# Two fused transformer blocks on one core: query norm and rotation on VectorE, low-rank queries behind their projection, and other heads' work in front of the diff heads' transposes in the last stage

## The chip, the core and the metric

The kernel runs on one core of one Trainium2 chip. The core has TensorE (PE, the matrix engine), VectorE (DVE), ScalarE (ACT), GpSimd (POOL) and SyncE (SP, which here only issues DMAs). Each engine runs its own list of instructions strictly in order and waits where an operand isn't there yet. The metric is the time of one execution on the device, in microseconds (us); lower is better. The kernel before takes 1979.63 us, the median of 3 runs (1977.76 to 1987.02).

## What is computed

A first block (gated linear attention, spatial gating, a PEER layer with 16 of 16384 experts for each of 8 heads) is followed by a second one, which takes its output as x, a context of 256 tokens, and two conditioning vectors. There are 256 tokens, a width of 1024 and one batch entry. The change is in the second block, of two layers (DEPTH_2 = 2), and there in the latent tokens x alone, not in the context tokens:

```python
mod = silu_c @ w_ada[l] + b_ada[l]             # shifts, scales and gates
h = _rms(x, g_attn_pre[l]) * (1.0 + sc_a) + sh_a
p = h @ w_in                                   # q_a, kv_a, dq, dk, dv, gq, gk, gv
q = (_rms(q_a, g_mla_q) @ w_mla_qb)            # MLA: 4 heads of 64 + 32, rank 256
kv = (_rms(c_kv, g_mla_kv) @ w_mla_kvb)
q_d = _rope(dq, rope_small)                    # diff: 4 heads of 2 x 32
q_g = _rope(_rms(gq, g_gqa_q), rope_large)     # GQA: 8 query heads of 64
k_g = _rope(_rms(gk, g_gqa_k), rope_large)     #      2 key heads
o = softmax(q @ [k, k_ctx].T * scale) @ [v, v_ctx]
d = _rms(o_diff[0] - lam * o_diff[1], g_diff_sub) * (1.0 - lam_init)
x = x + gt_a * _rms(concat(o_mla, d, o_gqa) @ w_out[l], g_attn_post[l])
hf = _rms(x, g_ffn_pre[l]) * (1.0 + sc_f) + sh_f
x = x + gt_f * _rms((silu(hf @ w_gate) * (hf @ w_up)) @ w_down, g_ffn_post[l])
```

`_rope` multiplies the two halves of a head, x1 and x2, with tables: (x1 c - x2 s, x2 c + x1 s). `_rms` divides by the root of the mean square and multiplies by the gain.

## The kernel before

**Stages.** The first block comes first, with the context's layer 0 beside its PEER stage. The last stage, from about 1182 us, is the latent tokens' layer 0 (beside it the ada vectors of layer 1 and the context's keys of layer 1) and then layer 1. In both, `split` and `rope` are true: every operand of a large matmul is split in two float32r numbers, a high and a low one (`whi` and `wlo` of a weight, made by a cast on ScalarE at L188 and a subtraction on VectorE at L190; `bTh` and `bTl` of an activation, L365 and L370), and three matmuls take the place of one (L206).

**A layer.** `layer` norms and transposes x (L385, L395), and then projects in four blocks: A of the keys (`w2a`), A of the queries (`w2c`, first half: q_a and dq), B of the queries (`w2c`, second half: gq, in tile `qB`), and B of the keys and values (`w2b`, tile `kB`, named `kBx` in the profile for the latent tokens). Between them stand the diff heads' rotations and stacked operands (`qdS`, `kdS`), the MLA's low-rank queries (`lowrank`: norm, transposes `lr` at L1015; the load of `wqb`; matmuls `qb` at L1184; rotation; transposes into `qmT`), the MLA's keys (`kvb`, transposes into `kmT`) and the GQA queries (`gqa`: norm, rotation, transposes into `qgT`). Then `attention` runs 4 diff heads beside 2 pairs of MLA heads and 4 pairs of GQA heads: S by matmul, its maximum on VectorE (L1231), exponential on ScalarE (L1233), transposes PT (L1261), products `pd` (L1296) or `po` (L1330). At the diff heads' end comes a norm on VectorE (`dd`, L1350 and L1351) and transposes `ddT` (L1355). The output projection (`w2o`), a norm with a gate row (broadcast by 8 matmuls `bc`, L349, to a row `gv`), and the FFN follow: 22 tiles `ft` of 128 hidden units, each with gate and up matmuls (`gu`) and down products (`f`) into four banks, one per token tile t and half b.

**Who does what.** `GQ_POOL = 1` puts the norm's multiplies (L1031 gain, L1032 rstd) and the rotation (L984 to L990) of the 8 GQA query heads on GpSimd in the split layers. The power in `rstd` (L320) is on GpSimd wherever it has at most 16 columns.

**What sets the order.** Each piece is a Python generator that yields an estimate of its time; `together` and `merge` always advance the one that is behind. `ORDER = 2` picks the branch of `kv_gen` in which the low-rank queries run beside projection B of the keys. The framework's scheduler then arranges each engine's instructions by its own model of their times, within the dependences; `pinned` forbids single matmuls to move ahead of another. DMAs of weights are issued on SP in order, into four buffers (`raw`); a load waits until the last reader of its buffer is done. The loads of `wqb`, the keys' and queries' weights, the ada weights and `w2o` share these four.

**The last products.** With `STAGF = 3` the down products of token tile 1 for the last three ft are held back to the end; there they run ft by ft, both banks of each.

## Time and profile before

| | |
|---|---|
| median of 3 runs | 1979.63 us (1977.76 to 1987.02) |
| profiled execution | 1979.57 us, span 1977.8 us |
| busy PE, DVE, ACT, POOL | 1532.2 (77%), 1461.5 (74%), 691.4 (35%), 596.7 us (30%) |
| mean granted clock of TensorE | 0.876 |
| layer 0 of the last stage | about 1182 to 1582 us |
| layer 1 of the last stage | about 1582 us to the end |
| the chain that ended last | PE 46%, DVE 24%, DMA 15%, issue 6%, POOL 3%, ACT 3% |

Busy times are sums over stages with different limits: in the middle of the program VectorE and the gathering DMAs set the pace, in the last stage TensorE does, but for a few stretches. A wait in a row below is the idle time of the engine before the instruction, and what ended it. `x4` behind a row is a count of instructions drawn together. On TensorE the granted clock is 1.00 where the whole stretch ran at 2.4 GHz; a stretch at 1.2 GHz counts half.

### The profile page before, as it was taken

The page shows a single profiled execution, that of the slowest core. Times are in us where ns is not written, and L with a number is a line of the kernel's source. Part 1 is how long each engine was busy: PE and PEld are TensorE (multiplying, and loading weights), DVE is VectorE, ACT ScalarE, POOL GpSimd, SP SyncE. Part 2 cuts the span into 40 slices and gives each one's busy share as a digit, 9 for nine tenths or more (in the row PEclk, how much of TensorE's full clock was granted, in tenths as well). Part 3 has the DMA queues.
Part 4 walks back from the last instruction along what each step waited for, and adds up shares of the span by engine and source line. Part 5 has one row for each costly group of instructions (what it writes and reads, how often), then busy time and mean ns, then how long its engine had stood idle before and what let it go on. Part 6 is the DMA issues. An engine that isn't in the chain of part 4 may idle for free.

```text
span 1977.8 us, 22950 instructions
## 1 busy us (share of the span) xinstructions
PE 1532.2 (77%) x7872; PEld 1163.4 (59%) x7872; DVE 1461.5 (74%) x2557; ACT 691.4 (35%) x1326; POOL 596.7 (30%) x626
## 2 busy tenths in 40 slices
PE   6889999996486665556655109799999997989997
PEld 3766767743344443334433008477988975769997
DVE  3756545999989999988888996665876567745554
ACT  2534433343343001000000106576444365754443
POOL 0000002675656566666656641200000004000000
PEclk8999999997577877777787659999999998999999
DMA  9849888999999999999999963614976442026552
GB/s 358 330 151 330 290 311 297 332 401 341 331 356 346 409 401 395 369 409 409 409 409 409 401 276 125 203 34 154 323 277 234 158 156 93 1 75 198 185 185 93
DMA packets 150183, 542.31 MB, mean 274 GB/s; under 512 B 16801, under 2 KB 17185, under 8 KB 150066
## 3 DMA queue, kind: packets, MB, share of 16 engines
q1 hardware_dynamic: 75152, 269.53, 38.5%
q0 software_dynamic: 73728, 268.47, 35.1%
q10 hardware_dynamic: 1186, 2.85, 0.4%
q8 instruction: 62, 1.02, 0.2%
q14 instruction: 55, 0.45, 0.1%
HBM read 539.73 MB, written 1.05 MB: 273 GB/s over the span
## 4 chain that ended last, share of the span: by engine, by line
PE 46%; DVE 24%; DMA 15%; issue 6%; POOL 3%; ACT 3%; SPq 0%; POOLq 0%; DVEq 0%; ACTq 0%
PE blk L206 15%; PE gu L206 12%; DVE h2p L811 7%; DVE row L913 7%; DMA row<-in_up,idx 6%; PE f L206 5%; DMA row<-in_down,idx 5%; PE S L206 2%; PE PT L1261 2%; PE po L1330 2%; DMA vraw<-in_w_ada 2%; PE ada L264 1%; POOL row L929 1%; PE qk L206 1%; DVE wlo L190 1%
## 5 line engine op out<-in xcount | busy, mean ns | idle before, releaser
L190 DVE TENSOR_TENSOR wlo<-raw,whi 128x1024 fp32r<-128x1024 f32 (+1 forms) x245 | 297.4, 1220 | 234.5 <-ACT whi L188 229.6
L188 ACT CAST whi<-raw 128x1024 fp32r<-128x1024 f32 (+1 forms) x245 | 254.2, 1044 | 315.9 <-PE blk L206 102.7
L811 DVE SCALAR_TENSOR_TENSOR h2p<-row,dot,h2p 128x1024 f32<-128x1024 f32 x254 | 326.6, 1286 | 22.5 <-DMA row<-in_up,idx 18.0
L913 DVE SCALAR_TENSOR_TENSOR row<-row,h2p 128x1024 f32<-128x1024 f32 x256 | 305.7, 1213 | 30.3 <-DMA row<-in_down,idx 28.9
L929 POOL DMA_INDIRECT row<-in_down,idx x256 | 242.5, 947 | 170.5 <-DMA row<-in_down,idx 33.0
L929 POOL DMA_INDIRECT row<-in_up,idx x256 | 244.4, 955 | 147.2 <-DVE h2p L811 50.8
L206 PE MATMUL f<-raw,hid 128*128 128x512 f32 x176 | 129.7, 905 | 196.1 <-DVE hid L1494 196.1
L320 POOL TENSOR_TENSOR ss<-ss,mhalf 128x1 f32<-128x1 f32 (+1 forms) x39 | 24.5, 630 | 714.2 <-DVE ss L318 713.9
L206 PEld LDWEIGHTS f<-raw,hid 128*128 128x128 f32 x176 | 50.4, 301 | 265.5 <-DVE hid L1494 204.9
L206 PE MATMUL gu<-bTh,whi 128*128 128x256 f32 x704 | 201.4, 286 | 4.1 <-ACT bTh L365 2.8
L206 PE MATMUL gu<-bTl,whi 128*128 128x256 f32 x704 | 201.2, 286 | 0.7 <-DVE bTl L370 0.7
L206 PE MATMUL gu<-bTh,wlo 128*128 128x256 f32 x704 | 200.7, 285 | 0.9 <-DVE wlo L190 0.9
L206 PE MATMUL gu<-bT,raw 128*128 128x256 f32 x704 | 155.4, 379 | 0.0
L206 PEld LDWEIGHTS gu<-bT,raw 128*128 128x128 f32 x704 | 133.8, 190 | 27.2 <-issue 10.2
L206 PEld LDWEIGHTS gu<-bTh,whi 128*128 128x128 f32 x704 | 136.1, 193 | 6.7 <-ACT bTh L365 3.4
L206 PEld LDWEIGHTS gu<-bTl,whi 128*128 128x128 f32 x704 | 136.1, 193 | 3.1 <-DVE bTl L370 1.5
L206 PEld LDWEIGHTS gu<-bTh,wlo 128*128 128x128 f32 x704 | 136.3, 194 | 2.7 <-DVE wlo L190 1.3
L1481 ACT ACTIVATE fth<-gu 128x256 f32<-128x256 f32 x66 | 25.0, 379 | 316.2 <-PE gu L206 316.2
L395 PE MATMUL nT<-cst,w 128*128 128x128 f32 x112 | 21.9, 357 | 103.8 <-DVE ss L318 75.9
L206 PE MATMUL blk<-wlo,hTh 128*128 128x512 f32 x224 | 90.2, 403 | 0.6 <-DVE wlo L190 0.6
L206 PE MATMUL blk<-whi,hTl 128*128 128x512 f32 x224 | 88.3, 396 | 0.0
L206 PE MATMUL blk<-whi,hTh 128*128 128x512 f32 x224 | 85.2, 403 | 2.6 <-ACT whi L188 2.6
(420 smaller groups left out, 3117.0 us busy)
## 6 DMA issues: line engine op xcount, KB each, us to landing
raw<-in_wgu SPq DMA_DIRECT2D x132, 512.0 KB, 5.1
araw<-in_w_ada SPq DMA_DIRECT2D x72, 512.0 KB, 5.7
raw<-in_wd SPq DMA_DIRECT2D x66, 512.0 KB, 5.1
raw<-in_w1b SPq DMA_DIRECT2D x56, 512.0 KB, 5.7
vraw<-in_w_ada SPq DMA_DIRECT2D x32, 512.0 KB, 5.3
raw<-in_w_ada SPq DMA_DIRECT2D x24, 512.0 KB, 4.6
raw<-in_w2c SPq DMA_DIRECT2D x24, 512.0 KB, 4.8
raw<-in_w2o SPq DMA_DIRECT2D x24, 512.0 KB, 3.8
```

Of the source, the lines that this page charges most:

```text
L188: nc.scalar.copy(hi[:, :n], raw[:, :n])
L190: nc.vector.tensor_sub(lo[:, :n], raw[:, :n], hi[:, :n].bitcast(F32))
L206: self.mm_last = self.nc.tensor.matmul(out, l, r, start=first and i == 0, stop=last and i == n - 1)
L264: mm = nc.tensor.matmul(ps[32 * j:32 * j + 32, :], lhs[:, k, :], raws[j // 2][:, j % 2 * 512:(j % 2 + 1) * 512], start=k == 0, stop=k == K ...
L320: nc.gpsimd.tensor_tensor(ss, ss, self.mhalf[:, :n], op=ALU.pow)
L395: nc.tensor.transpose(ps[:, q, t * P:(t + 1) * P], xn[t][:, k * P:(k + 1) * P], self.ident)
L811: self.slot = nc.vector.scalar_tensor_tensor(side, r, w, side, op0=ALU.mult, op1=ALU.add)
L913: self.slot = nc.vector.scalar_tensor_tensor(r, r, 1.0, self.side, op0=ALU.mult, op1=ALU.mult, accum_out=self.at(t, s))
L929: nc.gpsimd.indirect_dma_start(out=r, out_offset=None, in_=table, in_offset=bass.IndirectOffsetOnAxis(ap=self.idx[:, t, s:s + 1], axis=0))
L1261: nc.tensor.transpose(ps[:, j, :], pr[:, j * P:(j + 1) * P], self.ident)
L1330: nc.tensor.matmul(po[64 * i:64 * i + 64, :], vf(kvs[j // 2], j % 2, i), PTs[i][:, j, :], start=j == 0, stop=j == 2 * nk - 1)
L1481: nc.scalar.activation(th, ps[:, 0, :], AF.Tanh, scale=0.5)
```

## The change

All parts are in the last stage's two layers.

1. The GQA query norm and rotation run on VectorE. The gain is no longer multiplied in the norm: `gain_tables` multiplies it and the scale into the rotation's tables, in three operations a layer, and the rotation takes these tables.
2. `kv_gen` runs projection B of the queries, the low-rank queries (`mla` of the queries) and the diff queries side by side, and after that projection B of the keys, with the GQA keys behind it, beside the MLA keys and the GQA queries. Nothing of the projections is left to run beside the attention.
3. In `diff` a yield of 4.0 stands in front of the transposes `ddT`.
4. In layer 1 the broadcast of the gate row of the FFN stands behind the first part of the FFN's norm; before, it stood at the third FFN tile.
5. The held-back last products run bank by bank: nine matmuls for bank 0, then nine for bank 1.

On GpSimd, layer 1, the kernel before has these rows in the place of part 1 (numbers behind a name are buffers; `rr` is the reciprocal root, `w4` a scratch tile):

```order
L1031 TENSOR_TENSOR qB_10822<-qB_10822,gqs_11180 128x512 x2
L320 TENSOR_TENSOR rr_11183<-rr_11183,mhalf_81 128x16
L1032 TENSOR_TENSOR qB_10822<-qB_10822,rr_11183 128x512 x2
L984 TENSOR_TENSOR w4_11233<-qB_10822,cst_72 128x8x32
L986 TENSOR_TENSOR w4_11233<-qB_10822,cst_72 128x8x32
L984 TENSOR_TENSOR w4_11233<-qB_10822,cst_72 128x8x32
L986 TENSOR_TENSOR w4_11233<-qB_10822,cst_72 128x8x32
L988 TENSOR_TENSOR qB_10822<-qB_10822,cst_72 128x512 x2
L990 TENSOR_TENSOR w4_11232<-qB_10822,w4_11233 128x4x64 x4
```

All but the power are gone from there now. On VectorE, layer 1, the kernel after has (`sst` is the negated maximum of a row of S, which stands in `S`, and `kmTxl` the low part of the MLA's keys):

```order
L370 TENSOR_TENSOR kmTxl_11298<-tr_11306,kmTxh_11297 96x4x128
L1035 TENSOR_TENSOR qB_10822<-qB_10822,rr_11234 128x512 x2
L986 TENSOR_TENSOR w4_11286<-qB_10822,w4_11243 128x8x32
L988 TENSOR_TENSOR w4_11286<-qB_10822,w4_11243 128x8x32
L986 TENSOR_TENSOR w4_11286<-qB_10822,w4_11243 128x8x32
L988 TENSOR_TENSOR w4_11286<-qB_10822,w4_11243 128x8x32
L1256 TENSOR_REDUCE sst_11432<-S_11425 128x1
L1256 TENSOR_REDUCE sst_11448<-S_11445 128x1
L1256 TENSOR_REDUCE sst_11455<-S_11452 128x1
L990 TENSOR_TENSOR qB_10822<-qB_10822,w4_11243 128x512 x2
L1256 TENSOR_REDUCE sst_11477<-S_11470 128x1
L1348 RECIPROCAL rs_11436<-sst_11432 128x1
```

The operations on `qB` and `w4` have come in between the reductions of the first softmaxes, and the rstd multiply stands directly behind the keys' low part.

On TensorE, layer 0, between the keys' and values' projection and the first S of the MLA heads, the kernel before has (`ada` are the conditioning matmuls of layer 1, 4 for each pair of loads):

```order
L206 MATMUL blk1_7022<-whi_7211,bTl_6638 128x512
L1015 MATMUL lr_7167<-cst_72,w4_7157 128x128 x4
L996 MATMUL tr_7177<-cst_72,w4_7110 128x128 x4
L996 MATMUL tr_7184<-cst_72,w4_7110 128x128 x4
L1184 MATMUL qb_7192<-raw_7173,w4_7166 128x384 x2
L1184 MATMUL qb_7196<-raw_7173,w4_7166 128x384 x2
L264 MATMUL ada_7200<-raw_7203,lhs2_90 32x512 x2
L264 MATMUL ada_7200<-raw_7201,lhs2_90 32x512 x2
L996 MATMUL tr_7248<-cst_72,w4_7191 96x128 x4
L996 MATMUL tr_7255<-cst_72,w4_7191 96x128 x4
L1261 MATMUL PT_7285<-cst_72,prob_7271 128x128 x4
L206 MATMUL S_7361<-kmTxh_7122,qmTh_7246 128x256
```

and the kernel after, from the transposes of the GQA queries (`tr`, from `w4`) on:

```order
L998 MATMUL tr_7211<-cst_72,w4_7163 128x128 x4
L206 MATMUL S_7449<-kdSx_6812,qdS_6951 128x256
L206 MATMUL S_7449<-kdSxc_2840,qdS_6951 128x256
L998 MATMUL tr_7218<-cst_72,w4_7163 128x128 x4
L264 MATMUL ada_7225<-raw_7228,lhs2_90 32x512 x2
L264 MATMUL ada_7225<-raw_7226,lhs2_90 32x512 x2
L264 MATMUL ada_7225<-raw_7254,lhs2_90 32x512 x2
L264 MATMUL ada_7225<-raw_7252,lhs2_90 32x512 x2
L264 MATMUL ada_7225<-raw_7292,lhs2_90 32x512 x2
L264 MATMUL ada_7225<-raw_7290,lhs2_90 32x512 x2
L206 MATMUL S_7467<-kmTxh_7175,qmTh_7020 128x256
```

The `lr` and `qb` rows have moved ahead, into the projections, and six of the rows on `ada` now stand in one piece, of which the last two read the pair `raw_7292` and `raw_7290`, loaded into the buffers that the first pair frees.

On TensorE, layer 1, around the diff heads' transposes, the kernel before has

```order
L206 MATMUL S_12004<-kgTxcl_10737,qgTh_11297 128x256
L206 MATMUL S_12004<-kgTxch_10736,qgTl_11298 128x256
L1355 MATMUL ddT_11842<-cst_72,dd_11369 128x128 x4
L1261 MATMUL PT_11864<-cst_72,prob_11859 128x128 x4
L1261 MATMUL PT_11884<-cst_72,prob_11879 128x128 x4
```

and the kernel after

```order
L206 MATMUL S_12056<-kgTxch_10736,qgTl_11332 128x256
L206 MATMUL S_12077<-kgTxh_11388,qgTh_11331 128x256
L206 MATMUL S_12077<-kgTxl_11389,qgTh_11331 128x256
L206 MATMUL S_12077<-kgTxh_11388,qgTl_11332 128x256
L206 MATMUL S_12077<-kgTxch_10736,qgTh_11331 128x256
L206 MATMUL S_12077<-kgTxcl_10737,qgTh_11331 128x256
L206 MATMUL S_12077<-kgTxch_10736,qgTl_11332 128x256
L1383 MATMUL ddT_11904<-cst_72,dd_11397 128x128 x4
L1286 MATMUL PT_11925<-cst_72,prob_11920 128x128 x4
```

Ahead of `ddT` the kernel after has 18 matmuls of S in one piece (three softmaxes of the GQA heads), of which the first nine are not shown, and the transposes PT that stood behind it are partly ahead of it now. The broadcast of part 4 stands, as its eight matmuls `bc`, among the matmuls of layer 1's output projection, ahead of the norm's transposes.

The diff:

```diff
--- before.py
+++ after.py
@@ -973,12 +973,14 @@
     def w4(W, n):
         return W.tile([P, 1024], F32, tag="w4", name="w4", bufs=W4C if W.name == "Wc" else 7)[:, :n]
 
-    def rope(self, dst, src, H, hd, key, W, eng=None):
+    def rope(self, dst, src, H, hd, key, W, eng=None, tabs=None):
 
         eng = eng or self.nc.vector
         half = hd // 2
         cs = self.c("cs" if key == "s" else "cl").rearrange("p (t d) -> p t d", t=2)
         sn = self.c("ss" if key == "s" else "sl").rearrange("p (t d) -> p t d", t=2)
+        if tabs:
+            cs, sn = tabs
         t2 = self.w4(W, 1024).rearrange("p (t d) -> p t d", t=2)[:, :, :H * hd].rearrange("p t (h d) -> p t h d", h=H)
         for t in range(2):
             eng.tensor_tensor(t2[:, t, :, 0:half], src[:, t, :, half:hd],
@@ -1028,7 +1030,8 @@
             nc.vector.reduce_sum(rv[:, t, :], sq[:, t], axis=AX.X)
         self.rstd(rr, 2 * H, 64, tag)
         for t in range(2):
-            eng.tensor_tensor(src[:, t], src[:, t], g.unsqueeze(1).to_broadcast([P, H, 64]), op=ALU.mult)
+            if g is not None:
+                eng.tensor_tensor(src[:, t], src[:, t], g.unsqueeze(1).to_broadcast([P, H, 64]), op=ALU.mult)
             eng.tensor_tensor(src[:, t], src[:, t], rv[:, t, :].unsqueeze(2).to_broadcast([P, H, 64]), op=ALU.mult)
 
     def stack(self, W, src, order):
@@ -1135,6 +1138,11 @@
             yield from together(projB(), proj[1])
             yield from together(proj[2], mla())
             return chain(proj[3], gqa(), proj[4])
+        if split:
+
+            yield from together(proj[3], proj[2], proj[1])
+            yield from together(chain(projB(), gqa()), mla(), proj[4])
+            return iter(())
         yield from together(proj[2], proj[1])
         if ORDER == 1:
             yield from together(projB(), chain(mla(), proj[3]))
@@ -1195,31 +1203,48 @@
 
         def gqa():
             gq = qB.rearrange("p t (h d) -> p t h d", h=8)
+            if rope:
+                self.gqa_norm(W, gq, 8, None, f"gq{l}")
+                tabs = self.gain_tables(self.w4(W, 256), d["gq"])
+                yield 3.0
+                qg = self.w4(W, 1024).rearrange("p (t a k d) -> p t a k d", t=2, a=4, k=2)
+                self.rope(lambda t: [(qg[:, t, :, k, :], lambda z, k=k: z[:, 4 * k:4 * k + 4, :]) for k in range(2)],
+                          gq, 8, 64, "l", W, tabs=tabs)
+                yield 3.0
+                yield from self.queries_T(Q, q, qg)
+                return
             g = self.small.tile([P, 64], F32, tag="gqs", name="gqs", bufs=1)
             nc.vector.tensor_scalar(g, d["gq"], GQA_SCALE, None, op0=ALU.mult)
-            eng = nc.gpsimd if GQ_POOL and split else nc.vector
-            self.gqa_norm(W, gq, 8, g, f"gq{l}", eng)
+            self.gqa_norm(W, gq, 8, g, f"gq{l}")
             yield 3.0
 
             qg = self.w4(W, 1024).rearrange("p (t a k d) -> p t a k d", t=2, a=4, k=2)
 
-            def halves(k):
-                return lambda z: z[:, 4 * k:4 * k + 4, :]
-
-            if rope:
-                self.rope(lambda t: [(qg[:, t, :, k, :], halves(k)) for k in range(2)], gq, 8, 64, "l", W, eng)
-                yield 3.0
-            else:
-                for t in range(2):
-                    for k in range(2):
-                        nc.vector.tensor_copy(qg[:, t, :, k, :], gq[:, t, 4 * k:4 * k + 4, :])
-            q["qgT"] = qgT = self.operand(Q, [P, 4, T], "qgT", True)
-            for t in range(2):
-                self.put(qgT, lambda z: z[:, :, t * P:(t + 1) * P],
-                         self.transposed([qg[:, t, i].rearrange("p k d -> p (k d)") for i in range(4)], P))
-            yield 2.0
+            for t in range(2):
+                for k in range(2):
+                    nc.vector.tensor_copy(qg[:, t, :, k, :], gq[:, t, 4 * k:4 * k + 4, :])
+            yield from self.queries_T(Q, q, qg)
 
         return projA, diff, projB, mla, gqa
+
+    def gain_tables(self, room, g):
+
+        nc = self.nc
+        tb = room.rearrange("p (i t d) -> p i t d", i=2, t=2)
+        for i, (n, cuts) in enumerate((("cl", ((0, 64, 0),)), ("sl", ((0, 32, 32), (32, 64, 0))))):
+            src = self.c(n).rearrange("p (t d) -> p t d", t=2)
+            for lo, hi, at in cuts:
+                nc.vector.scalar_tensor_tensor(
+                    tb[:, i, :, lo:hi], src[:, :, lo:hi], GQA_SCALE,
+                    g[:, at:at + hi - lo].unsqueeze(1).to_broadcast([P, 2, hi - lo]), op0=ALU.mult, op1=ALU.mult)
+        return tb[:, 0], tb[:, 1]
+
+    def queries_T(self, Q, q, qg):
+        q["qgT"] = qgT = self.operand(Q, [P, 4, T], "qgT", True)
+        for t in range(2):
+            self.put(qgT, lambda z: z[:, :, t * P:(t + 1) * P],
+                     self.transposed([qg[:, t, i].rearrange("p k d -> p (k d)") for i in range(4)], P))
+        yield 2.0
 
     def softmax(self, W, lhs, keys, nk):
 
@@ -1349,6 +1374,9 @@
             self.rstd(ss, 8, 64, f"ds{l}")
             nc.vector.tensor_tensor(ddf, ddf, ss.unsqueeze(2).to_broadcast([P, 8, 64]), op=ALU.mult)
             nc.vector.tensor_tensor(ddf, ddf, d["dsub"].unsqueeze(1).to_broadcast([P, 8, 64]), op=ALU.mult)
+            if st["split"]:
+
+                yield 4.0
             ps = self.pst([P, 2, 2, P], "ddT")
             for f in range(2):
                 for t in range(2):
@@ -1443,7 +1471,12 @@
         yield 3.0
 
         fT = self.operand(W, [P, KD, T], "bT", split)
-        drain(self.norm_T(x, cc[:, 2, :], m[:, 24:32], fT, "f"))
+        norm = self.norm_T(x, cc[:, 2, :], m[:, 24:32], fT, "f")
+        next(norm)
+        if split and l == 1:
+
+            gv = self.bcast_row(self.scratch(), cc[:, 3, :])
+        drain(norm)
 
         norm_ins = None
         if split:
@@ -1497,8 +1530,8 @@
             def down(ft, hid):
                 wd = self.weight(a["wd"][l, ft], U, split)
 
-                def products(t, ft=ft, hid=hid, wd=wd):
-                    for b in range(2):
+                def products(t, bs=range(2), ft=ft, hid=hid, wd=wd):
+                    for b in bs:
                         self.mm(banks[t][b], self.pairs(self.sl(hid, lambda z: z[:, t * P:(t + 1) * P]),
                                                         self.sl(wd, lambda z: z[:, b * 512:(b + 1) * 512])),
                                 ft == 0, ft == NFT - 1)
@@ -1517,7 +1550,7 @@
                         yield BACK
                     ahead = this
             for ft in range(NFT if split else 0):
-                if ft == GVFT:
+                if ft == GVFT and l == 0:
                     gv = self.bcast_row(self.scratch(), cc[:, 3, :])
                 with self.pinned(norm_ins):
                     self.upto(vec, VN)
@@ -1528,9 +1561,10 @@
                 if ft < NFT - STAGF:
                     later.pop()(1)
                 elif ft == NFT - 1:
-                    with self.pinned(self.mm_last if STAGF else None):
-                        for f in later:
-                            f(1)
+                    for b in range(2):
+                        with self.pinned(self.mm_last):
+                            for f in later:
+                                f(1, (b,))
                 if side and ft >= SIDE_FT:
                     with self.pinned(norm_ins):
                         next(side[0], None)
```

## Rows read from the trace of the kernel before

**Rows 1.** busy: PE, PEld, DVE, ACT, POOL; clock; DMA, by stretch
```profile
1230.00:1250.00 20.00, 14.95 (x71) 9.96 (x73) 15.54 (x35) 9.34 (x21) 16.49 (x15) 1.00 0.19 60
1250.00:1275.00 25.00, 19.31 (x131) 12.28 (x132) 14.64 (x47) 10.21 (x25) 1.02 (x1) 0.86 0.70 232
1643.00:1665.00 22.00, 15.16 (x56) 10.07 (x55) 16.89 (x35) 10.63 (x23) 16.39 (x14) 0.77 0.31 106
1665.00:1690.00 25.00, 19.28 (x125) 17.73 (x124) 19.34 (x58) 16.39 (x41) 1.01 (x1) 0.80 0.06 22
```

**Rows 2.** waits of TensorE, layer 0: total us, times, longest
```profile
PE ada L264 <- DMA raw<-in_w_ada: 6.3, 5, 3.3
...
PE lr L1015 <- DVE w L1009: 1.4, 2, 0.9
```

**Rows 3.** waits of TensorE, layer 1
```profile
PE lr L1015 <- DVE w L1009: 4.5, 1, 4.5
...
PE tr L996 <- DVE kBx L990: 2.8, 1, 2.8
...
PE tr L996 <- POOL w L990: 2.3, 2, 2.0
...
PE ddT L1355 <- DVE dd L1351: 2.2, 1, 2.2
...
PE S L206 <- ACT prob L1233: 2.0, 3, 1.7
```

**Rows 4.** timeline of TensorE, qb in layer 0, then 1 (start, us)
```profile
1247.22 2.75 PE L1184 MATMUL qb<-raw,w 128*128 128x384 f32 x8
...
1660.54 4.71 PE L1184 MATMUL qb<-raw,w 128*128 128x384 f32 x8
```

**Rows 5.** timeline of GpSimd, layer 1, the power
```profile
1643.29 2.90 POOL L320 TENSOR_TENSOR rr<-rr,mhalf 128x16 f32<-128x16 f32 x1
```

**Rows 6.** VectorE groups by shape (busy us, mean ns | idle)
```profile
L1388 DVE TENSOR_TENSOR w<-blk,w 128x512 f32<-128x512 f32 x8 | 5.5, 689 | 15.2 <-ACT junk L1387 15.1
...
L988 DVE TENSOR_TENSOR qA<-qA,cst 128x256 f32<-128x256 f32 x4 | 1.7, 425 | 0.1
...
L984 DVE TENSOR_TENSOR w<-w,cst 128x64 f32<-128x64 f32 x4 | 0.9, 226 | 3.5 <-ACT w L1185 3.5
```

**Rows 7.** timeline of VectorE, layer 0, then layer 1
```profile
1233.77 0.21 DVE L1286 SCALAR_TENSOR_TENSOR nls<-nls,sst,nlam 128x1 f32<-128x1 f32 x1
...
1240.76 1.15 DVE L1286 SCALAR_TENSOR_TENSOR nls<-nls,sst,nlam 128x1 f32<-128x1 f32 x1
...
1241.83 2.45 DVE L1009 SCALAR_TENSOR_TENSOR w<-qA,ss,lrows 128x256 f32<-128x256 f32 x2
...
1654.41 0.86 DVE L1009 SCALAR_TENSOR_TENSOR w<-qA,ss,lrows 128x256 f32<-128x256 f32 x2
```

**Rows 8.** busy from kvB to kBx, columns as Rows 1
```profile
1640.70:1678.10 37.40, 24.89 (x116) 18.04 (x114) 30.22 (x75) 18.21 (x41) 19.70 (x16) 0.82 0.27 91
1228.70:1268.10 39.40, 28.66 (x161) 17.39 (x159) 28.73 (x72) 16.63 (x39) 18.72 (x16) 0.96 0.48 159
```

**Rows 9.** ada in layer 0: the longest wait, and section 6
```profile
1266.27 1.94 PE L264 MATMUL ada<-raw,lhs 128*32 128x512 f32 x8 [3.33 <-DMA raw<-in_w_ada]
...
raw<-in_w_ada SPq DMA_DIRECT2D x24, 512.0 KB, 4.6
```

**Rows 10.** chain of waits, layer 1: projection, later broadcast
```profile
1750.35 10.94 PE blk L206 x48
...
1789.14 0.89 PE bc L349 x8
```

**Rows 11.** chain of waits, the end of layer 1
```profile
1961.52 5.07 PE f L206 x21
...
1966.67 0.70 ACT junk L1387 x2
```

## The prediction

> **What bounds the kernel now.** I read the page's 40 slices first, then busy time by stretch, then TensorE's waits, then the timelines of the two stretches that the change touches. The last stage is two latent layers, from about 1182 to 1582 us and from 1582 to the end. In both the FFN, and most of the attention, keep TensorE busy nearly all the time; an edit there gains only if it takes work off TensorE or fills a hole. The holes lie between the projections and the first softmaxes. [rows 1] shows them: in layer 0 TensorE works 14.95 of 20 us and then 19.31 of 25, in layer 1 15.16 of 22 and 19.28 of 25, with the granted clock at 0.77 and 0.80 in layer 1, a mean over time at 2.4 GHz and time at 1.2. That is 10.7 us idle in layer 0 and 12.6 in layer 1. In the same stretches GpSimd works 16.49 and 16.39 us and VectorE is at 15.54 of 20 and 16.89 of 22, so VectorE is nearly as loaded as TensorE.
>
> [rows 2] and [rows 3] say what TensorE waited for. Layer 0: 6.3 us for the ada loads, 1.4 us for the low-rank operand (lr), and for the diff heads' ddT the same 2.2 us as in layer 1, where the row reads the same word for word. Layer 1: 4.5 us for lr, 2.3 us for GpSimd's rotated queries, 2.8 us for kBx, 2.2 us for ddT, 2.0 us for exponentials that free a bank for the next S. When the clock falls, the same eight qb matmuls take 4.71 us in layer 1 against 2.75 in layer 0 [rows 4].
>
> The profiled execution took 1979.57 us (span 1977.8 and 1.8 around it), 0.06 us from the median of the runs, so I sum against 1979.57. One half of a per cent, 9.9 us, is about what a measurement of this kernel can tell from no change.
>
> **Query norm and rotation on VectorE.** GpSimd loses its two gain multiplies, two rstd multiplies and twelve rotation operations per layer. It keeps the 16-wide power, 2.90 us [rows 5], on which the rstd multiplies still wait. VectorE gains four operations of 128x512 at 0.689 us (two rstd, two cosine products), eight of 128x256 at 0.425, and three table operations [rows 6]: 4 x 0.689 + 8 x 0.425 = 6.2 us, and for the tables two at 0.226 and one between 0.226 and 0.425, together 0.8. So 7.0 us per layer on VectorE replace about 16 on GpSimd. The cover that hid the GpSimd time is other engines' work; VectorE's 7.0 us have no such cover, because S waits for VectorE's reductions.
>
> VectorE also gets something back. While GpSimd worked, a pair of L1009 operations took 2.45 us and an L1286 1.15; elsewhere they take 0.86 and 0.21 [rows 7]. That is 2.5 us in these two places; I take 2.5 per layer, and 0 as the other end. From the kvB projection's end to the first transposes of kBx VectorE was busy 30.22 of 37.4 us in layer 1 and 28.73 of 39.4 in layer 0 [rows 8]. After the change this is 30.2 + 7.0 - 2.5 = 34.7 and 33.2. So if VectorE were packed without a gap, layer 1 could gain 2.7 us up to there and layer 0 6.2; with no give-back 0.2 and 3.7. The order shows these operations among the reductions of the first softmaxes, and the rstd multiplies in front of them wait for the power with those reductions queued behind. That costs up to 2.9 us per layer, so the other end is a loss of 2.9. For layer 1 I take -1.4, midway between 0.2 and 2.7.
>
> The give-back has a rule in the Trainium skill, "SBUF — State Buffer", section "Who interferes with whom": a VectorE instruction with two SBUF inputs and a GpSimd instruction that reads SBUF exclude each other for the whole of an instruction. [rows 7] agrees in size. By it the whole stretching would leave with GpSimd's work, and the sum takes the end with 2.5. Against the change speaks another page of the Trainium skill, "GPSIMD Engine Reference", section "4.1 Engine selection", which puts GpSimd at about twice VectorE's time for two inputs: by it 16.4 us would become 8.2 rather than 7.0, and the room in layer 1 1.5 rather than 2.7 us.
>
> **Low-rank queries right after projection A.** No instruction is added. The lr transposes and the qb matmuls leave the hole and stand inside the kvB projection, which TensorE would do anyhow; the wqb load moves up SP's queue, and it holds one of the four raw slots until qb, so the fourth kvB load waits for qb. This removes the waits for lr: 1.4 us in layer 0, up to 4.5 in layer 1. But these are the same idle time that VectorE's bound above gives back; I don't count it twice. In layer 0 the order now has the matmuls of three ada pairs in one piece behind the query transposes. The third pair loads into slots that the first frees, and a load takes 4.6 us to land [rows 9]. TensorE has nothing in front of it for that time, where before S and PT matmuls stood between the pairs; one such wait cost 3.33 us even so [rows 9]. It ends up to 4.6 us later, against an earlier arrival by the lr wait and a backlog on VectorE that drains meanwhile. Ends: +4.6 and -6.2; I take -1.0, most of the 1.4 us of the lr wait, as the ada waits remain whatever VectorE does.
>
> **Other heads in front of ddT.** TensorE idled 2.2 us in each layer [rows 3]. In layer 1 the order now has eighteen S matmuls directly ahead, behind the last products of the diff heads. They are half as wide as the projection's, which take 10.94 us for 48 [rows 10], so 0.114 us each and 2.1 us in all: about the wait. Ends are 0 and -4.4 for both. What is late next is the bank for S, freed by an exponential, which already cost 2.0 us in layer 1 [rows 3]; I take half of that off: -3.4.
>
> **Broadcast of the gate row in layer 1.** The words of the code put it after the norm's start, but the order has its eight matmuls inside the output projection, ahead of the hole. TensorE is busy there without a pause, 48 matmuls in 10.94 us, as it is at the old place in the FFN, where half of the broadcast takes 0.89 us [rows 10]. So 1.8 us of work go from one full stretch to another: 0, with -1.8 if the projection waits there for its weights' casts, and +1.4 if its two copies (0.70 us each by ScalarE's square of 128x512 in [rows 11]) delay the norm.
>
> **Last products by bank.** The last 21 matmuls take 5.07 us, 0.24 each; ScalarE's squares of the two banks follow, the first pair of rows 0.70 us [rows 11]. With bank 0 complete nine matmuls (2.2 us) before the end, its square lies beside them: -0.7 in layer 1. In layer 0 side work follows, so -0.3, between 0 and -0.7. Together -1.0.
>
> Sum: -1.4 - 1.0 - 3.4 + 0 - 1.0 = -6.8, that is 1979.57 - 6.8 = 1972.8 us.
>
> **Rivals.**
> A, the holes close: VectorE's chain gets short enough that lr 4.5, tr 2.3, kBx 2.8 and the slow clock's 1.96 (4.71 - 2.75) in layer 1 go, lr 1.4 in layer 0, ddT 4.4, the tail 1.4 and the broadcast 1.8: -20.6, 1959 us. For it: 23 us of idle time in the two holes, and a higher clock if TensorE is fed. Against it: VectorE's load [rows 8] and the ada loads. Chance 0.28.
> B, VectorE's queue becomes the bound: the power's 2.9 us stop it in both layers with the key operand kmTl and the reductions behind, the third ada pair costs 4.6 in layer 0, the clock stays low for 1.0 us more, and S in front of ddT waits for VectorE and ScalarE as ddT did: 5.8 + 4.6 + 1.0 - 1.0 (tail) = +10.4, 1990 us. It decides as soon as VectorE reaches the rstd multiply more than 1 us before the power is done. For it: the in-order queue. Against it: operations that wait for the reduction itself stood there before as well, and lr work moved out of the way. Chance 0.10.
> C, the wait only changes its name: TensorE waits as long for VectorE as for GpSimd, and half of the ddT gain goes to the exponentials: -1.7 - 1.0 = -2.7, 1977 us. Chance 0.20.
>
> **Numbers.** My forecast has 0.42, with its own range 1967 to 1977. Faster by over 0.5% is below 1969.7: nearly all of A and over a quarter of the forecast, 0.28 + 0.12 = 0.40. Slower by over 0.5% is above 1989.5: half of B and the tail of an unforeseen stall, 0.10 with what the ends above allow. The remaining 0.50 is no change. The range that leaves out about 0.2 is 1957 to 1985, with the lower part of A and most of B outside.
>
> **What would show it.** Right: no PE wait for POOL; lr waits gone; ddT under 0.6 us in both layers; GpSimd near 3 us in each hole; VectorE's L1009 at 0.86 a pair; TensorE's waits in the holes now for kmTl, sst or kBx, and in layer 0 one of 3 to 5 us for the third ada pair; the output projection of layer 1 longer by the broadcast's 1.8 us and its FFN shorter by it. Wrong: layer 1's clock at 1.00 and its hole shorter by over 5 us (A), or VectorE idle behind the power and both holes longer (B).

## The result: slower by 1.0%, and the profile after

The changed kernel takes 1999.70 us, the median of 5 runs (1994.15 to 2006.90), against 1979.88 for the kernel before in the same comparison: a ratio of 1.0096 [1.0066, 1.0125]. A later comparison of the same two gave 1.0111 [1.0093, 1.0130]. The prediction, 1972.8 us and a range to 1985, was wrong in sign.

The page of the changed kernel (1 core, profiled execution 2000.12 us; lines of code stand 2 to 34 further down than before: L1231, L1233, L1261, L1351 and L1355 are now L1256, L1258, L1286, L1376 and L1383):

```profile
span 1998.4 us, 22925 instructions
...
PE 1543.6 (77%) x7872; PEld 1172.7 (59%) x7872; DVE 1462.0 (73%) x2585; ACT 693.0 (35%) x1326; POOL 565.6 (28%) x598
```

GpSimd lost 31.1 us, as it should (596.7 before). TensorE was busy 11.4 us longer, though its work did not grow. Where: busy time by stretch, of before and then of after, each from a layer's first norm transposes; layer 0's stretch ends at the gate row's broadcast behind the attention, layer 1's at the FFN's norm. The columns are those of [rows 1]: length; busy time and instructions of PE, PEld, DVE, ACT and POOL; TensorE's granted clock; the DMAs' share and rate.

```profile
1185.70:1350.00 164.30, 149.25 (x891) 115.21 (x892) 101.31 (x238) 107.70 (x233) 23.64 (x22) 0.96 0.38 124
1596.10:1768.60 172.50, 151.86 (x866) 123.41 (x867) 109.42 (x245) 107.19 (x232) 24.94 (x22) 0.93 0.22 71
```

```profile
1182.40:1362.70 180.30, 161.28 (x896) 123.95 (x897) 102.07 (x253) 108.97 (x234) 8.56 (x8) 0.88 0.35 113
1612.00:1791.10 179.10, 157.26 (x883) 127.35 (x882) 109.45 (x259) 107.77 (x232) 8.57 (x8) 0.90 0.22 68
```

Layer 0 lost 16.0 us and layer 1 6.6: nearly the whole loss lies here (the whole last stage lost 23.8 us, the stages before it were 3.3 shorter). Of these 22.6 us only 5.2 are idle time of TensorE (15.05 to 19.02, and 20.64 to 21.84). The other 17.4 are busy time for about the same matmuls, 1.8 of it the broadcast moved here. The clock column says why: a clock of 0.96 means that twice the missing 0.04 of the stretch, some 13 of 164.3 us, ran at 1.2 GHz; at 0.88 it is some 43 of 180.3 us. In layer 1 it went from 24 to 36 us. A second profile of the changed kernel, run e13_after below, has 17.8 us more than before in the two stretches, 5.6 of them idle, and by the same working 67 us at 1.2 GHz, against 37 before and 79 in the first.

TensorE's waits in layer 0 and then in layer 1 (total us, times, longest), to be read against [rows 2, 3]:

```profile
PE ddT L1383 <- DVE dd L1376: 4.7, 1, 4.7
PE ada L264 <- DMA raw<-in_w_ada: 4.3, 1, 4.3
PE S L206 <- ACT prob L1258: 3.9, 3, 2.5
PE S L206 <- DVE kmTxl L370: 2.6, 1, 2.6
```

```profile
PE S L206 <- ACT prob L1258: 5.6, 3, 2.8
...
PE ddT L1383 <- DVE dd L1376: 4.5, 1, 4.5
...
PE kvb L1101 <- ACT w L1018: 2.6, 1, 2.6
```

The waits for lr and for GpSimd's queries are gone, and so is that for kBx. In their place stand new ones (for the MLA keys' kmTxl, for kvb's operand) and longer ones for banks, freed by the exponentials, and ddT, which was to lose its 2.2 us, waits twice as long. The timeline of TensorE at ddT in layer 0 (start, us, instructions, in brackets the idle time before and its releaser):

```profile
1315.23 0.61 PE L1321 MATMUL pd<-kBxc,w 128*128 128x64 f32 x4
1315.77 0.38 PE L206 MATMUL S<-kgTxcl,qgTh 64*128 64x256 f32 x1
...
1317.91 0.28 PE L206 MATMUL S<-kgTxch,qgTl 64*128 64x256 f32 x1
1322.88 1.11 PE L1383 MATMUL ddT<-cst,dd 128*128 128x128 f32 x4 [4.69 <-DVE dd L1376]
```

and VectorE in the same time:

```profile
1315.88 0.28 DVE L1323 TENSOR_SCALAR dd<-pd,nls 128x64 f32<-128x64 f32 x1 [0.74 <-PE pd L1321]
1316.31 0.69 DVE L1256 TENSOR_REDUCE sst<-S 128x1 f32<-128x512 f32 x1
...
1318.57 0.41 DVE L1373 TENSOR_REDUCE ssd<-w 128x4 f32<-128x256 f32 x1
1318.90 0.68 DVE L1256 TENSOR_REDUCE sst<-S 128x1 f32<-128x512 f32 x1
1319.49 0.16 DVE L318 TENSOR_SCALAR ssd<-ssd 128x8 f32<-128x8 f32 x1
1321.40 0.69 DVE L1375 TENSOR_TENSOR dd<-dd,ssd 128x512 f32<-128x512 f32 x1 [1.75 <-POOL ssd L320]
1322.13 0.69 DVE L1376 TENSOR_TENSOR dd<-dd,lrows 128x512 f32<-128x512 f32 x1
```

Behind the last pd stand twenty S matmuls and nothing else, and they last 2.4 us; ddT, next in its queue, needs a chain of 7.0 us through VectorE and GpSimd, in which four reductions of S matmuls stand among the norm's own steps. Before, fourteen products po stood there besides six S, which lasted 2.8 us, and the chain took 5.0 us, with one such reduction in it. So most of the 2.5 us by which the wait grew is the longer chain. The rows of before:

```profile
1302.88 0.61 PE L1296 MATMUL pd<-kBxc,w 128*128 128x64 f32 x4
...
1304.13 1.24 PE L1330 MATMUL po<-w,vmxc 128*64 128x256 f32 x7
...
1308.47 0.63 PE L1355 MATMUL ddT<-cst,dd 128*128 128x128 f32 x4 [2.20 <-DVE dd L1351]
```

The clock in the changed kernel there, in windows of 5 us:

```profile
1318.00:1323.00 5.00, 0.31 (x3) 0.13 (x2) 3.04 (x7) 0.00 (x0) 1.64 (x1) 0.77 0.00 0
1323.00:1328.00 5.00, 5.00 (x22) 3.59 (x24) 1.47 (x7) 2.94 (x7) 0.00 (x0) 0.55 0.26 72
1328.00:1333.00 5.00, 5.00 (x35) 3.27 (x32) 2.48 (x7) 5.00 (x13) 0.00 (x0) 1.00 0.00 0
```

TensorE did nearly nothing, and the work behind it ran mostly at 1.2 GHz: 22 matmuls in 5 us, against 35 in the next 5.

### The profile page after: what moved, and what is told of

Its sections match the earlier page's. It is cut to its first block, busy times and chain, and to the rows that moved or that the text cites. A ratio compares the mean times of both kernels' runs of the same rounds, so it can differ in the third digit from the quotient of the medians.

```text
span 1998.4 us, 22925 instructions
## 1 busy us (share of the span) xinstructions
PE 1543.6 (77%) x7872; PEld 1172.7 (59%) x7872; DVE 1462.0 (73%) x2585; ACT 693.0 (35%) x1326; POOL 565.6 (28%) x598
## 4 chain that ended last, share of the span: by engine, by line
PE 46%; DVE 26%; DMA 14%; issue 6%; ACT 4%; POOL 2%; DVEq 0%; SPq 0%; POOLq 0%; ACTq 0%
PE blk L206 14%; PE gu L206 12%; DVE row L913 8%; DVE h2p L811 7%; DMA row<-in_up,idx 6%; PE f L206 5%; DMA row<-in_down,idx 5%; PE S L206 2%; PE PT L1286 2%; PE po L1355 2%; PE ada L264 1%; DMA vraw<-in_w_ada 1%; POOL row L929 1%; PE pd L1321 1%; DVE wlo L190 1%
## 5 line engine op out<-in xcount | busy, mean ns | idle before, releaser
L206 PEld LDWEIGHTS gu<-bT,raw 128*128 128x128 f32 x704 | 133.9, 190 | 27.4 <-issue 10.4
L395 PE MATMUL nT<-cst,w 128*128 128x128 f32 x112 | 22.6, 363 | 103.9 <-DVE ss L318 75.6
```

Source lines behind the costliest of these rows:

```text
L206: self.mm_last = self.nc.tensor.matmul(out, l, r, start=first and i == 0, stop=last and i == n - 1)
L395: nc.tensor.transpose(ps[:, q, t * P:(t + 1) * P], xn[t][:, k * P:(k + 1) * P], self.ident)
```

## The experiments

The parts are numbered as in the section on the change. Each ratio is against the kernel before, in runs on the same chip. Runs of one kernel scatter: the kernel before ran from 1971.78 to 1989.59 us in 34 runs on one chip. So one profile shows a mechanism, and the ratio what it costs.

### Which part

The first question: part 1's queue on VectorE (rival B of the prediction), part 2, or separate stalls that add up, each from its own part?

**Part 3 undone.**

```diff
-            if st["split"]:
-
-                yield 4.0
```

> The changed kernel without its part 3 (no yield in front of the diff heads' transposes). In the changed kernel's profile ddT waits 4.7 and 4.5 us where it waited 2.2 and 2.2 before, with the granted clock of the following 5 us at 0.55 in layer 0. Theory (three separate stalls, each with a wait and a stretch at 1.2 GHz behind it): the two waits fall to 2 to 3 us and the time by about 8 us, from 1999.7 to 1992. Rival R1 (the clock is low through the whole attention once it has fallen in the hole before it, so one stall more or less is nothing): under 3 us, 1997 to 2000. Rival R2 (the projections' order, part 2, is the whole loss): 0 to 2 us.

Measured: 1997.39 us, 1.0078 [1.0049, 1.0107]. ddT still waits 4.5 us in each layer: the yield neither makes the wait nor takes it away.

**Part 1 undone, but for the tables.** The norm's multiplies and the rotation are on GpSimd again.

```diff
-                self.gqa_norm(W, gq, 8, None, f"gq{l}")
+                self.gqa_norm(W, gq, 8, None, f"gq{l}", nc.gpsimd)
-                          gq, 8, 64, "l", W, tabs=tabs)
+                          gq, 8, 64, "l", W, nc.gpsimd, tabs=tabs)
```

> The changed kernel with the query norm's multiplies and the rotation back on GpSimd (the tables with the gain folded in stay). In the changed kernel VectorE stands 2.28 us in front of the rstd multiply until the power is done, S then waits 2.6 us for kmTxl, and ScalarE 5.7 us for the first maximum; TensorE runs at 1.2 GHz from 1247 to 1257 us. Theory: these go in layer 0 and partly in layer 1, 8 us, from 1999.7 to 1992. Rival R1: the hole keeps another stall (the third ada pair, 4.3 us) and with it the low clock: under 3 us. Rival R2: 0 to 2 us. Rival R3 (GpSimd's longer chain is now waited for by the ada matmuls that stand behind its transposes): slower, by up to 5 us.

Measured: 1998.02 us, 1.0073 [1.0046, 1.0100]. Two of its waits, layer 1:

```profile
PE S L206 <- ACT prob L1258: 9.6, 3, 8.3
...
PE ddT L1383 <- DVE dd L1376: 4.5, 1, 4.5
```

Nothing is regained. By itself this does not clear part 1, as GpSimd's longer chain brings waits of its own (4.9 us for tr in layer 0); the next run does, which keeps part 1.

**Part 2 undone.**

```diff
-        if split:
-
-            yield from together(proj[3], proj[2], proj[1])
-            yield from together(chain(projB(), gqa()), mla(), proj[4])
-            return iter(())
```

> The changed kernel with the order of the projections and low-rank queries of before (part 2 undone). Theory: the wait for the third ada pair (4.3 us) and the one for kvb's operand in layer 1 (2.6 us) go, but lr's waits (1.4 and 4.5 us) come back: 9 us at most, 1991 to 1996. Rival R1: the clock falls at another stall of the same holes: under 3 us. Rival R2 (part 2 is the whole loss): to 1980.

Measured: 1977.39 us, 0.9980 [0.9956, 1.0005]. In layer 1 the old wait is back, and ddT is below its 2.2 us:

```profile
PE lr L1017 <- DVE w L1011: 5.1, 1, 5.1
...
PE ddT L1378 <- DVE dd L1371: 1.9, 1, 1.9
```

Parts 1, 3, 4 and 5 are all in this kernel, and it is level with before.

**Parts 1 and 3 undone together** (both edits above).

> The changed kernel without parts 1 and 3, so parts 2, 4 and 5 alone (with the gain folded into the tables). Theory: the two gains add, 16 us, 1984. Rival R1: once both are gone the clock stays up and more comes back than the sum of the two alone, to 1978 or less. Rival R2: 1996 to 2000.

Measured: 1997.32 us, 1.0083 [1.0054, 1.0111]. Part 2 is the whole loss; the theory of stalls that add up fell.

**Parts 3 and 5 alone, on the kernel before** (the yield, and the last products bank by bank).

```diff
+            if st["split"]:
+
+                yield 4.0
             ps = self.pst([P, 2, 2, P], "ddT")
-                        for f in later:
-                            f(1)
+                    for b in range(2):
+                            for f in later:
+                                f(1, (b,))
```

> The kernel before with parts 3 and 5 alone. The changed kernel without part 2 took 1977.4 us against 1981.3 of before. If the little gain there came from ddT and the last products: 1977. If it came from the rotation on VectorE: 1981.

Measured: 1978.78 us, 0.9997 [0.9978, 1.0016]: no difference.

### Which half of part 2

Part 2 brings the low-rank queries forward, and it leaves nothing `late`: the GQA keys, which ran at the head of the other heads' chain beside the diff heads, now come before the attention.

**Low-rank queries forward, GQA keys late as before.**

```diff
-            yield from together(chain(projB(), gqa()), mla(), proj[4])
-            return iter(())
+            yield from together(projB(), mla(), proj[4])
+            return gqa()
```

> The changed kernel with only the first half of part 2: the low-rank queries beside projection B of the queries, the GQA keys' norm and transposes left as work that runs beside the attention. So far part 2 as a whole costs about 20 us (with it 1997 to 2000, without it 1977). Theory T1 (the loss comes with the empty rest: the GQA keys are pulled in front of the attention and all heads start together, so that the diff heads end with nothing but S in front of ddT): this kernel is near 1980, ddT waits about 2 us. Rival T2 (the loss comes with the low-rank queries in front: wqb's buffer, the kvB weights and so the MLA keys come late, and three ada pairs in one piece): near 1997.

Measured: 1984.05 us, 1.0014 [0.9995, 1.0033]; ddT waits 1.9 us in each layer. T2 falls as the cause of the whole loss.

**Nothing late, low-rank queries where they were.**

```diff
-            yield from together(proj[3], proj[2], proj[1])
-            yield from together(chain(projB(), gqa()), mla(), proj[4])
+            yield from together(proj[2], proj[1])
+            yield from together(chain(projB(), gqa()), chain(mla(), proj[3]), proj[4])
             return iter(())
```

> The changed kernel with only the second half of part 2: nothing is left to run beside the attention, the low-rank queries stand behind the MLA keys as before. T1: near 1997, ddT waits 4 to 5 us in both layers. T2: near 1980. If both halves cost, 1985 to 1992 in each.

Measured: 1992.72 us, 1.0052 [1.0031, 1.0072]. This is neither T1's 1997 nor T2's 1980; ddT waits 3.0 and 4.0 us. TensorE idles less than before in the two stretches (13.5 and 19.6 us against 15.1 and 20.6), and still it is slower. The profile (the longest of its 11 runs, 2001.44 us) shows one way, in layer 1; windows of 3 us, columns as above:

```profile
1696.00:1699.00 3.00, 2.46 (x19) 2.05 (x18) 2.96 (x7) 3.00 (x8) 0.00 (x0) 1.00 0.00 0
1699.00:1702.00 3.00, 2.42 (x16) 2.29 (x16) 2.92 (x9) 2.56 (x7) 0.00 (x0) 0.82 0.00 0
1702.00:1705.00 3.00, 3.00 (x13) 2.66 (x13) 1.11 (x4) 1.19 (x4) 0.00 (x0) 0.50 0.03 5
...
1720.00:1723.00 3.00, 3.00 (x15) 2.88 (x14) 0.97 (x2) 1.36 (x4) 0.00 (x0) 0.50 0.00 0
...
1732.00:1735.00 3.00, 1.45 (x7) 1.15 (x6) 1.76 (x5) 0.00 (x0) 0.67 (x1) 0.50 0.00 0
1735.00:1738.00 3.00, 0.52 (x3) 0.53 (x4) 1.39 (x2) 0.00 (x0) 0.97 (x1) 0.50 0.00 0
1738.00:1741.00 3.00, 3.00 (x12) 1.91 (x11) 0.86 (x2) 1.88 (x5) 0.00 (x0) 0.50 0.00 0
1741.00:1744.00 3.00, 3.00 (x21) 2.01 (x19) 0.65 (x2) 3.00 (x7) 0.00 (x0) 0.85 0.02 5
```

After two windows with half a microsecond idle in each, TensorE is at 1.2 GHz for 39 us. For the first 30 of them, to 1732, it is busy all the time; then it waits 4.0 us for ddT. Reading waits alone, one would not find the loss of those 30 us.

### Is it the missing delay, or the keys' place?

With nothing late, the other heads start level with the diff heads. If that is the cause, a rest of 3.0 (the planner's units), which adds no instruction, must take the loss back.

**A rest of 3.0 in the place of the late keys**, all of part 2 otherwise.

```diff
-            return iter(())
+            return iter((3.0,))
```

> The changed kernel as it is, all of part 2, but with a rest of 3.0 units that does nothing, handed to the attention as the late work: the heads other than the diff heads are laid 3.0 later, as far as the GQA keys' work put them before. With part 2's first half alone, where that work was left, the time was 1984; with all of it 1998 to 2000. If the loss of the second half is that all heads start together: 1984 to 1988, ddT waits 2 us again. If it is that the GQA keys' work stands in front of the attention: 1997 to 2000.

Measured: 1995.42 us against 1990.71 on this, a slower, chip: 1.0011 [0.9990, 1.0032]. Its waits for ddT and for banks in layer 0, which were 4.7 and 3.9 us in the changed kernel:

```profile
PE S L206 <- ACT prob L1258: 2.7, 4, 1.9
...
PE ddT L1383 <- DVE dd L1376: 2.2, 1, 2.2
```

**The changed kernel again, the next three beside it.**

> The changed kernel itself, on the same chip as the next three, as their zero. Expected at 1.007 to 1.010 of before.

Measured: 2000.77 us, 1.0111 [1.0093, 1.0130].

**A rest of 6.0** (`iter((6.0,))`).

> The changed kernel with a rest of 6.0 units that does nothing as the late work, where 3.0 gave 1.0011 of before and none 1.0096. If the distance between the diff heads and the others is what counts and 3.0 was not yet enough: 0.997 to 1.000 of before, ddT waits under 2 us. If 3.0 was enough and the low-rank queries in front cost the rest: 1.001. If the two values so far were chips and not kernels: as the zero.

Measured: 1985.42 us, 1.0027 [1.0006, 1.0048]. This is well below the zero, but no better than 3.0; ddT waits 2.2 us, not under 2.

**Low-rank queries where they were, a rest of 3.0** (the second half of part 2 as above, `iter((3.0,))`).

> The changed kernel with the second half of part 2 alone (GQA keys' work ahead of the attention, low-rank queries behind the MLA keys as before; 1.0052 of before), and the rest of 3.0. If the start of the other heads is all of that half's loss: 0.998 as without part 2. If the GQA keys' work ahead of the attention costs by itself: 1.003 or more.

Measured: 1975.94 us, 0.9985 [0.9966, 1.0005].

**Part 2 undone, a rest of 3.0 more in front of the late keys.**

```diff
-            return gqa()
+            return chain(iter((3.0 if split else 0.0,)), gqa())
```

> The changed kernel without part 2 (0.998 of before) and a rest of 3.0 more in front of the GQA keys' work that is late there. If more distance helps in general: 0.993 to 0.996. If there is an optimum near the 3.0 that the GQA keys' work itself takes: 0.998 to 1.003.

Measured: 1988.24 us, 1.0044 [1.0026, 1.0062], above both expectations.

The ratios to the kernel before, put together (each comparison on one chip, but not all on the same; the changed kernel stands in two):

| | GQA keys late, as before | nothing late | nothing late, rest of 3.0 |
|---|---|---|---|
| low-rank queries as before | 0.9980 | 1.0052 | 0.9985 |
| low-rank queries forward | 1.0014 | 1.0096, 1.0111 | 1.0011 |

So the loss of the second half is the missing delay, and not the keys' place: the left and the right column agree. It is 0.7% with the low-rank queries as before and 0.8 to 1.0% with them forward, and a rest that does nothing takes it back. The low-rank queries forward are the smaller part: 0.3% in the outer columns, where the intervals overlap, and 0.4 to 0.6% with nothing late, where those of 1.0052 and 1.0111 lie apart. With 3.0 more than the late keys give, the kernel loses again (0.4%), though ddT waits no longer than before (2.2 us in each layer). A rest changes the order of the whole attention, so why more distance loses is open.

### Is it the clock?

If the clock lost behind ddT is what costs, useless work on TensorE in the wait must gain, though it makes the wait itself no shorter. In these kernels the added transposes write into a bank that the real ones overwrite.

**36 useless transposes in front of ddT in each layer of the changed kernel.**

```diff
+            for i in range(36 if st["split"] else 0):
+                nc.tensor.transpose(ps[:, i % 4 // 2, i % 2, :], sq[:, ...], self.ident)
```

> The changed kernel with 36 transposes more on TensorE in each layer, of the diff heads' squares into the bank that ddT overwrites: about 4 us of work without use that stands in the wait for ddT and nothing else. Theory C (what a stall costs is the wait and also the 1.2 GHz that follow it): ddT starts at the same time, the granted clock of the 5 us behind it rises from 0.55 towards 1, and the time falls by 2 to 4 us, to 1996. Rival C2 (the clock behind ddT falls for another reason, or the time there is VectorE's and ScalarE's): no change or slower by up to 4 us.

Measured: 1991.61 us, 1.0052 [1.0031, 1.0073], against 1.0096 and 1.0111 without them, in other comparisons. ddT comes 10.7 us behind the last pd in layer 0, where it came after 7.0, and yet the kernel is faster. Windows at its ddT in layer 0:

```profile
1320.00:1325.00 5.00, 5.00 (x33) 3.77 (x33) 3.50 (x10) 3.18 (x8) 1.64 (x1) 1.00 0.00 0
1325.00:1330.00 5.00, 5.00 (x44) 4.01 (x43) 1.78 (x3) 0.19 (x1) 0.00 (x0) 1.00 0.21 72
```

But the edit did more than fill the wait. The framework's scheduler, which arranges by its model of the times, laid other heads' work in front of ddT as well, in both layers: sixteen products po and eight transposes PT, where the changed kernel had S matmuls alone.

```profile
1318.65 0.61 PE L1321 MATMUL pd<-kBxc,w 128*128 128x64 f32 x4
...
1324.10 4.04 PE L1382 MATMUL ddT<-cst,w 128*128 128x128 f32 x35
...
1328.78 1.24 PE L1355 MATMUL po<-w,kBxc 128*64 128x256 f32 x7
1329.94 0.66 PE L1385 MATMUL ddT<-cst,dd 128*128 128x128 f32 x4
```

So this run does not tell what the useless work gains from what the new order gains. In its two stretches TensorE idles 32.4 us (40.9 in the changed kernel) and is at 1.2 GHz for 53 us (79).

**The same where part 2 is undone:** 16 in front of ddT, and 30 in the wait for lr in layer 1.

```diff
+            for i in range(16 if st["split"] else 0):
...
         ps = self.pst([P, nf, 2, P], "lr")
+        if tag == "q1" and self.hilo is not None:
+            with self.pinned(self.mm_last):
+                for i in range(30):
+                    nc.tensor.transpose(ps[:, i % 4 // 2, i % 2, :], src[:, ...], self.ident)
```

> The changed kernel without part 2 (1977.4 us against 1981.3 of before), and with transposes without use on TensorE: 16 in each layer's wait for ddT, and 30 (3.6 us) in layer 1's wait for lr, of the unnormed queries into the bank that lr overwrites. In the kernel without part 2 that wait is 5.1 us, and the clock of the stretch from kvb to kBx is 0.82. Theory C (a stall costs its length and then the time at 1.2 GHz behind it): TensorE does more, the waits end when they did, the clock in layer 1 from kvb to kBx is over 0.95, and the time falls by 4 to 8 us, to 1972. Rival C2 (the time there is VectorE's, and TensorE's clock only follows): the time stays at 1977, whatever the clock.

Measured: 1992.44 against 1990.71 us, 1.0005 [0.9983, 1.0027].

**The same on the kernel before.**

> The kernel before with the same transposes without use, 16 in each wait for ddT and 30 in layer 1's wait for lr (4.5 us there). Theory C: 1975, 4 to 8 us under before. C2: 1981.

Measured: 1997.77 against 1990.71 us, 1.0020 [0.9993, 1.0047].

**Only the 30 for lr, part 2 undone.**

> As e9, but with the 30 transposes in layer 1's wait for lr alone. Theory C: most of e9's gain, 1974, since that wait is the longer one. If the gain is behind ddT: 1977.

Measured: 1988.07 against 1990.71 us, 0.9987 [0.9963, 1.0012].

Theory C's 4 to 8 us came in none of the three, though the waits for lr (5.1 and 4.5 us) are as long as the changed kernel's for ddT. In the profile the filling does what it should: from kvb to the first transposes of kBx in layer 1, with part 2 undone and then with the 30 transposes too,

```profile
1632.90:1664.70 31.80, 21.21 (x101) 15.71 (x99) 28.02 (x81) 16.20 (x37) 3.07 (x2) 0.81 0.26 83
1655.00:1684.60 29.60, 22.32 (x130) 17.20 (x129) 27.59 (x81) 16.80 (x38) 3.16 (x2) 0.92 0.29 90
```

the clock rises from 0.81 to 0.92 and the stretch is 2.2 us shorter. That is 0.1% of the program, less than a ratio here can tell. As a recipe, filling waits with useless work is not shown to pay.

What all 18 profiles show together (the kernel before, the changed one and the sixteen runs): by the working above, the two stretches take 336 to 359 us, with 34 to 81 us at 1.2 GHz and 26 to 45 us idle. The length goes with the time at 1.2 GHz (correlation 0.93) more than with the idle time (0.72). That is where the time went; it does not say what lowered the clock in one order and not in another.

## Why the prediction was wrong, step by step

**The step that failed** is the price of part 2. Its only term, "Low-rank queries right after projection A", is for the first half, at -1.0 us. That nothing of the projections is left to run beside the attention has no term: it was put at nothing without a reason. The prediction asked what the moved instructions gain where they land, not what they leave behind. Part 2 with everything else in place costs 1.0096 or 1.0111 against 0.9980 without it, some 23 to 26 us. Of this the second half is the larger share: the chain beside the diff heads loses its head start, which costs 0.7% alone (some 14 us) and 0.8 to 1.0% with the first half, and comes back with a rest. The term that was priced came out with the wrong sign: 0.3% (5 to 7 us, intervals that overlap) where the head start is kept, 0.4 to 0.6% where it is not. What that part consists of is open.

**Other heads in front of ddT**, -3.4: eighteen S matmuls were to cover 2.2 us. In layer 0 it is twenty and they last 2.4 us, but they took the place of 2.8 us of work that covered before, and their reductions go in front of dd on VectorE: 4.7 and 4.5 us of waiting came in the place of 2.2 and 2.2. This belongs to part 2 (1.9 us without it, with the same yield). Even there the yield saved 0.3 us of 2.2 at most.

**The clock** has no term in the forecast's sum; rival A had it as a gain of 1.96 us and rival B as a loss of 1.0. In the pair of profiles 17.4 us of 22.6 are longer busy time, 15.6 without the broadcast; with the second profile of the changed kernel it is 10.4 of 17.8. The runs give less: in 34 runs of the kernel before, the mean granted clock lies between 0.866 and 0.880, and time falls by about 1.1 us for each 0.001. The medians of after and before on one chip are 0.866 and 0.875, which by that line is 10 of 21.5 us. So about a half to 0.7 of the loss is clock, as an estimate.

**Rival B** had the right sign, and its mechanism is in layer 0. VectorE reaches the rstd multiply 2.28 us before the power is done, and the key operand is behind it:

```profile
1244.01 1.29 DVE L1035 TENSOR_TENSOR qB<-qB,rr 128x512 f32<-128x512 f32 x2 [2.28 <-POOL rr L320]
1245.22 0.68 DVE L370 TENSOR_TENSOR kmTxl<-tr,kmTxh 96x512 fp32r<-96x512 f32 x1
```

S then waits 2.6 us for kmTxl. In layer 1 nothing waits for the power. But it isn't the cause. The kernel without part 2 has part 1 too; there VectorE does not wait for the power in either layer, and the kernel is level with before. With part 1 undone these 2.6 us go, and others come (tr for GpSimd, 4.9). That B's 1990 us lie nearest to the measured time is in part luck: the loss is not the sum of its terms. Rival C's thought, that a wait changes its name, holds for part 1.

**What came out as worked out.** VectorE's new work, by shape:

```profile
L992 DVE TENSOR_TENSOR w<-qB,w 128x256 f32<-128x256 f32 x8 | 3.0, 411 | 0.0
L1035 DVE TENSOR_TENSOR qB<-qB,rr 128x512 f32<-128x512 f32 x4 | 2.6, 684 | 2.3 <-POOL rr L320 2.3
L990 DVE TENSOR_TENSOR qB<-qB,w 128x512 f32<-128x512 f32 x4 | 2.6, 680 | 0.0
...
L1011 DVE SCALAR_TENSOR_TENSOR w<-qA,ss,lrows 128x256 f32<-128x256 f32 x4 | 1.8, 478 | 0.0
```

With the other products and the tables it is 6.5 us a layer, against 7.0. (GpSimd had ten rotation operations a layer, as its rows in the section on the change show, not twelve; the sum for VectorE does not use that count.) The give-back came too: the scaling of the low-rank queries takes 0.48 us each, where a pair took 2.45 beside GpSimd's work [rows 7]. The Trainium skill's rule in "SBUF — State Buffer", section "Who interferes with whom", agrees again (0.96 us a pair, with GpSimd's work gone). The third ada pair was to cost up to 4.6 us; it waits 4.30, once, and all ada waits together fell from 6.3 to 4.3. The FFN of layer 1, with the program's end, is 1.9 us shorter, about the broadcast's 1.8; the output projection's stretch did not show them (54.7 us from ddT to the FFN's norm in both).

**Last products by bank** gained nothing in layer 1, where -0.7 was expected. [rows 11] was misread: its 21 matmuls are not the last. The chain leaves TensorE for the square of bank 0, and three matmuls of bank 1 run beside that square:

```profile
1966.67 0.60 ACT L1387 ACTIVATE junk<-f 128x512 bf16<-128x512 f32 x1 [2.28 <-PE f L206]
1966.86 0.39 PE L206 MATMUL f<-whi,hidl 128*128 128x512 f32 x1
```

So the square already lay beside matmuls. From the end of the last matmul to the end of the program it is 10.5 us now and 10.6 before.

**A sign to read with care:** the first transposes of kBx came 0.1 and 1.4 us earlier into the layers than before, near the -1.4 of the prediction. But 342 matmuls stand in front of them in layer 0, where 370 stood; the point itself had moved in the order.

No version beats the kernel before beyond doubt: the best two, part 2 undone and the one with the rest but the old low-rank queries, are at 0.9980 and 0.9985, with intervals that touch 1.

## What to carry to other kernels

When a change empties a slot that ran beside other work, price the empty slot: it may have been what kept two chains apart. Work put in front of a waiting instruction is poor cover if its consumers stand in front of what that instruction waits for, on another engine (7.0 us against 5.0 here). And compare TensorE's busy time for the same matmuls before and after: a loss through the clock stands in no list of waits.

## What was not expected of the hardware

- Once at 1.2 GHz, TensorE stayed there for 39 us (1702 to 1741 us above), busy without a pause in the first 30. Behind the ddT wait of layer 0 it was back at 1.00 within 10 us. What decides between the two is open.
- Seventy-two useless transposes, with the order that the scheduler made of them, left the changed kernel faster (1.0052 against 1.0096 and 1.0111).
- GpSimd's power takes 2.91 us on 16 columns and 1.64 on 8.
